# One root chain for two pieces of 256 tokens: 20 pairs of head norms in a hybrid decoder layer on one core

## The chip, the core and the metric

The kernel runs on one core of one Trainium2 chip. The metric is the device time of one execution in microseconds (us): the median of 3 runs is 1681.12 us (1680.39 to 1683.96).

## What is computed

One decoder layer over 2048 tokens of width 1024, in fp32. The normalised input is projected at once into the columns of five head groups (A: spatial gating, B: forgetting attention, C: mLSTM, D: RWKV-7, M: attention into 256 memory tokens), each group is mixed along the tokens, gated, and all are projected back. Four of the five use RMS norms over heads of 64 columns:

```python
def rms_norm(x, g):
    xf = x.astype(jnp.float32)
    y = xf * lax.rsqrt(jnp.mean(xf * xf, axis=-1, keepdims=True) + EPS)
    return (y * g.astype(jnp.float32)).astype(x.dtype)

q = rms_norm(to_heads(q), q_g)          # groups B and M; k likewise
v = rms_norm(to_heads(gelu(v)), norm_g) # group A
h = sigmoid(o_logit) * h                # group C, the mLSTM's output
return rms_norm(h, out_g).reshape(bsz, seq, GROUP_W)
```

With 4 heads of 64 in each group, a piece of 256 tokens (two blocks of 128 on the partitions, 256 columns each) needs 8 roots per partition: 2 blocks by 4 heads.

## The kernel before, in words

**Work.** The tokens go in four quarters q of 512 (Q). Weights come by DMA (tile wraw) and are split by ScalarE and VectorE into a high and a low fp32r half (wt); the input comes the same way (xr, then ht). A projection is 3 matmuls for each of 8 slices of 128 rows. `proj_tok` (line 647) makes one piece of 256 tokens in one PSUM bank (tag pj): 48 matmuls, shown as pj<-wt,ht 128x256. `proj_tok2` (634) makes both pieces side by side in two banks, 96 matmuls. `proj_T` (600) makes transposed tiles, shown as pj<-ht,wt 128x512, 24 matmuls per bank. There are 3 pj banks until about 942 us and 2 behind that.

**Order of the work.** The program is written by Python generators. A projection calls `tick()` after every few matmuls; a tick moves each generator in the crowd `evac` (class at line 86) by one step and each lane (RWKV front and back, mLSTM, gates, attention) by its rate, for the mLSTM 0.8 steps per tick. `evac.add(g, kind)` lets at most two generators of a kind live; for a third it ticks the crowd, without matmuls, until one has ended. Until about 942 us (L235 in the rows) the framework's scheduler then orders the instructions of each engine; behind that (L373) the kernel's own recorder does, by a list schedule (`flush`, 307). On every engine the instructions run in the order that results.

**The head norms.** `head_norm` (733) is one generator per piece: ScalarE squares the piece (tile sq), VectorE (DVE) sums each head's 64 squares (TENSOR_REDUCE rs<-sq), scales and adds eps (TENSOR_SCALAR rs<-rs), and `rsqrt` (487) takes the roots: a first guess by integer arithmetic (rq<-rs) and three Newton rounds of three instructions each on the tiles rq, the last one writing rs. These are 11 instructions on 8 columns, each waiting for the one before. After three more steps the caller multiplies the piece by the roots.

**Its four callers.** `qk_post` (748) for Bk, Bq and Mq: the piece is copied from its bank into a tile yn (2 buffers), normed, transposed by TensorE (wk<-ident,yn, 4 matmuls), copied back into yn with the gain, and stored (qk_Bk<-yn and so on). `mem_keys`, one piece, goes the same way. `gate_values` (1050) norms the two pieces of gv. `mlstm_block` (1964) norms its output H (tile to) after chunk 1 and after chunk 3, then transposes it (wk<-ident,to) and multiplies it into cgz. All in all 41 chains: 16 of Bk and Bq, 8 of Mq, 1 of the memory keys, 8 of gv, 8 of the mLSTM.

**Around the end of a quarter** `group_B` (983) runs Bz, Bv, Bk, Bq. During Bq the next quarter's input is reloaded and split (xr<-hbd, ht), and the next quarter begins with `proj_T` of Cqk0. Bq's copies into yn need the two buffers that Bk's pieces held until their stores.

Of the kernel before, what the change touches and what calls it, by code (L numbers as in the profile page):

```python
# [9 lines left out]
F32 = mybir.dt.float32  # L10
F32R = mybir.dt.float32r
I32 = mybir.dt.int32
AF = mybir.ActivationFunctionType
ALU = mybir.AluOpType
AX = mybir.AxisListType
# [3 lines left out]
P = 128  # L19
# [4 lines left out]
HD = 64  # L24
# [3 lines left out]
EPS = 1e-6  # L28
Q = 512
# [35 lines left out]
class Lane:  # L65


    def __init__(self, rate=1.0):
        self.q, self.rate, self.due = deque(), rate, 0.0
# [390 lines left out]
def body(ctx: ExitStack, tc, x, xT, mem, memT, wp, wkv, wout, pv, wa, sguT, sgub, out, dbg=None):  # L460
    nc = rec = Recorder(tc.nc, tc)
# [25 lines left out]
    def rsqrt(t):  # L487

        n, b = t.shape[0], t.base_partition() if callable(t.base_partition) else t.base_partition
        y, u = (cp.tile([P, 16], F32, tag=f"rq{i}", bufs=1, name="rq")[b:b + n, :t.free_size()] for i in range(2))  # L490
        V.tensor_scalar(y.bitcast(I32), t.bitcast(I32), -0.5, 1597463007.0, op0=ALU.mult, op1=ALU.add)
        for o in (y, y, t):
            V.tensor_tensor(u, y, y, op=ALU.mult)
            V.scalar_tensor_tensor(u, u, -0.5, t, op0=ALU.mult, op1=ALU.mult)
            V.scalar_tensor_tensor(o, u, 1.5, y, op0=ALU.add, op1=ALU.mult)
# [234 lines left out]
        yield free  # L730
        then()

    def head_norm(pt, n, eps, pool=None):

        sq = pool.tile([P, 3 + Q], F32, tag="cext", bufs=2, name="sq") if pool else xp.tile([P, 512], F32, tag="sq", bufs=2, name="sq")
        A.activation(sq[:, :n], pt, AF.Square)
        yield
        m = n // HD
        r = xp.tile([P, 8], F32, tag="rs", bufs=4, name="rs")
        V.tensor_reduce(r[:, :m], sq[:, :n].rearrange("q (u x) -> q u x", x=HD), axis=AX.X, op=ALU.add)  # L740
        V.tensor_scalar(r[:, :m], r[:, :m], 1.0 / HD, eps, op0=ALU.mult, op1=ALU.add)
        rsqrt(r[:, :m])
        yield
        yield
        yield
        return r[:, :m].rearrange("q (u o) -> q u o", o=1).to_broadcast([P, m, HD])

    def qk_post(y, scale, d):

        r = yield from head_norm(y, 512, EPS)  # L750
        y3 = y.rearrange("q (u x) -> q u x", x=HD)
        V.tensor_tensor(y3, y3, r, op=ALU.mult)
        yield
        pt = bank()
        for p in range(2):
            for ii in range(2):
                T.transpose(pt[:, (2 * p + ii) * P:(2 * p + ii + 1) * P], y[:, ii * 256 + p * P:ii * 256 + (p + 1) * P], ident)
        A.activation(y, pt, AF.Copy, scale=scale)
        yield
        SY.dma_start(d.rearrange("p q t -> q p t"), y.rearrange("q (p t) -> q p t", p=2))  # L760

    def qk_cols(wt, hts, scale, dst, pts=None):
        def post(pt, d):
            y = xp.tile([P, 512], F32, tag="yn", name="yn")
            A.copy(y, pt)
            yield FREE
            yield from qk_post(y, scale, d)

        for i in range(0, 4, 2):
            evac.add(post(pts[i // 2] if pts else proj_tok(wt, hts, i), dst(i)), "yn")  # L770

# [233 lines left out]
    for q in range(NQ):  # L1005
        tok = slice(q * Q, (q + 1) * Q)
        hts = got()


        lanes["mlstm"].drain()  # L1010
        qk, gz = [None] * 4, []
        va = sp.tile([P, 4, NH, HD + 1], F32, tag="va", bufs=1, name="va")
        G.memset(va[:, :, :, HD:HD + 1], 1.0)
        to = sp.tile([P, 4, 256], F32, tag="to", bufs=1, name="to")
        for nm in GC:
            wt = W(nm)
            for j in range(2):
                if nm == "Cv":
                    A.copy(va[:, 2 * j:2 * j + 2, :, 0:HD].rearrange("q i u x -> q (i u) x"), proj_tok(wt, hts, 2 * j).rearrange("q (u x) -> q u x", x=HD))
                    evac.held -= 1  # L1020
                elif nm == "Co":
                    A.activation(to[:, 2 * j:2 * j + 2].rearrange("q i x -> q (i x)"), proj_tok(wt, hts, 2 * j), AF.Tanh, scale=0.5)
                    evac.held -= 1
                elif nm == "Cz":
                    gz.append(sp.tile([P, Q], F32, tag=f"cgz{j}", bufs=1, name="cgz"))
                    evac.add(gate(proj_T(wt, j, hts), gz[j]))
                else:
                    m = 2 * (nm == "Cqk1") + j
                    qk[m] = sp.tile([P, Q], F32, tag=f"qk{m}", bufs=1, name="qk")
                    evac.add(conv(proj_T(wt, j, hts), m, qk[m]))  # L1030
        lanes["mlstm"].q.append(evac.then(mlstm_block(nc, q, sp, xp, bank, ident, qk, va, to, gz, mcol, cdb, nmd, wid, cst, hp2, mixd[2], head_norm)))
        group_B(q)


# [12 lines left out]
        V.scalar_tensor_tensor(o, t_, 1.0, pt, op0=ALU.add, op1=ALU.mult)  # L1047
        yield FREE

    def gate_values(pt, o):  # L1050
        yield from gelu2(pt, o)
        v3 = o.rearrange("q (u x) -> q u x", x=HD)
        r = yield from head_norm(o, 512, 4 * EPS)
        V.tensor_tensor(v3, v3, r, op=ALU.mult)

    def spatial(pt, u_, gv, p, d):
# [44 lines left out]
    for q in (NQ - 1, 0, 1, 2):  # L1101
        tok = slice(q * Q, (q + 1) * Q)
        if q < NQ - 1:
            hts = got()
            group_M(q)
        if q == NQ - 1:
            while ahead and next(ahead[-1][2], ahead) is not ahead:
                pass
            while evac.all or any(l.q for l in lanes.values()):
                evac.tick()  # L1110
                for l in lanes.values():
                    l.step()
            csp.close()
            rctx.close()
            psx.close()
            ps = psx.enter_context(tc.tile_pool(name="ps2", bufs=1, space=PSUM))
            nbank = {"pj": 2, "wk": 3, "p2": 2, "acc": 1}
            rec.start()
            ctx.enter_context(tc.manual_schedule())
            att.open()  # L1120

            fu = [Unit(att, True, h, g) for h in range(NH) for g in range(NQ)]
            mu = [Unit(att, False, h, g) for g in range(NQ) for h in range(NH)]
            lanes["fox"].q.append(att.run(fu[:-1] + mu[:NH] + fu[-1:] + mu[NH:]))
            sp = cw.enter_context(tc.tile_pool(name="sp2", bufs=1))
            stage.update(pool=sp, bufs=2, raw=4, lag=2)
            wop = cw.enter_context(tc.tile_pool(name="wop", bufs=1))

            sgw = mp.tile([P, NH, P], F32, name="sgw")
            SY.dma_start(sgw, sguT)  # L1130
            G.affine_select(sgw, sgw, pattern=[[0, NH], [1, P]], compare_op=ALU.is_ge, fill=0.0, base=0, channel_multiplier=-1)
            sgb = mp.tile([P, 2, 1, P], F32, name="sgb")
            for p in range(2):
                for h in range(2):
                    SY.dma_start(sgb[64 * h:64 * h + 64, p, 0, :], sgub[2 * p + h:2 * p + h + 1, :].to_broadcast([64, P]))
            V.tensor_scalar(sgb, sgb, 0.25, None, op0=ALU.mult)


        wt = W("Av")
        gv = sp.tile([P, 2, 512], F32, tag="gv", name="gv")  # L1140
        for i in range(2):
            evac.add(gate_values(proj_tok(wt, hts, 2 * i), gv[:, i]), "gl")
        wt = W("Au")
        gu = []
        for p in range(2):
            gu.append(sp.tile([P, 512], F32, tag=f"gu{p}", name="gu"))
            evac.add(gelu2(proj_T(wt, p, hts), gu[p]), "gl")
        wt = W("Az")
        if q == NQ - 1:
            evac.add(mem_rstd(), "gl")  # L1150
        pts = proj_T2(wt, hts, send(load_mem, "mem_g", NMEM) if q == NQ - 1 else reload(q + 1) if q != NQ - 2 else None)
        for p in range(2):
            evac.add(spatial(pts[p], gu[p], gv, p, mixd[0][p][:, tok]), "gl")
        if q == NQ - 1:
            hm = got()
            evac.add(mem_keys(proj_tok2(W(0), hm, None, 2)[0]), "yn")
            evac.add(mem_values(proj_tok2(W(1), hm, reload(0), 2)[0]), "gl")
# [803 lines left out]
    A.copy(mcol.rearrange("q k x -> q (k x)"), pt[:, 0:192])  # L1961


def mlstm_block(nc, q, sp, xp, bank, ident, qk, va, to, gz, mcol, cdb, nmd, wid, st, hp2, mixd, head_norm):

    V, A, G, T, SY = nc.vector, nc.scalar, nc.gpsimd, nc.tensor, nc.sync
    tokq = slice(q * Q, (q + 1) * Q)
# [19 lines left out]
    for c in range(4):  # L1987
# [48 lines left out]
            V.tensor_tensor(H4[:, h], num[:, h, :, 0:64], dn[:, h].to_broadcast([P, 2, HD]), op=ALU.mult)  # L2036
        V.scalar_tensor_tensor(H[:, c], to[:, c], 1.0, hr, op0=ALU.add, op1=ALU.mult)
        if c % 2:
            h2 = H[:, c - 1:c + 1].rearrange("q c x -> q (c x)")
            h3 = h2.rearrange("q (u x) -> q u x", x=HD)  # L2040
            r = yield from head_norm(h2, 512, 4 * EPS, sp)
            V.tensor_tensor(h3, h3, r, op=ALU.mult)
        yield
    yield
    for p in range(2):
        pt = bank()
# [67 lines left out]
```

## Time and profile before

| | |
|---|---|
| median of 3 runs | 1681.12 us |
| profiled execution, own time / span | 1675.38 us / 1673.7 us |
| TensorE matmul (PE) busy | 1607.7 us, 96% of the span |
| VectorE (DVE) busy | 1198.6 us, 72% |
| ScalarE (ACT) busy | 858.0 us, 51% |
| GpSimd (POOL) busy | 316.5 us, 19% |
| mean granted TensorE clock | 0.988 |
| chain that ended last, by engine | PE 71%, DVE 13%, DMA 8% |

Busy time says how full an engine is, not whether anyone waits for it. The views used further down are: busy time by stretch of the span (with the granted TensorE clock), the list of who waited for whom, the summary of one tile's instructions, and single instructions in order of time, where a bracket at the end gives the idle time of the engine before the instruction and what ended it. The tile names in the rows carry no buffer numbers.

### The profile page before, as it was taken

How to read it: one execution, taken by the hardware profiler on the slowest of the kernel's cores; microseconds unless marked ns; L12 is line 12 of the kernel's file. 1: busy time of each engine (PE TensorE's matmuls, PEld its weight loads, DVE VectorE, ACT ScalarE, POOL GpSimd, SP SyncE). 2: the span in 40 equal slices, each digit the busy share in tenths (PEclk: the TensorE clock that was granted, in tenths of full speed). 3: DMA queues.
4: the chain of work that ended last, by engine and by line, in shares of the span. 5: the costliest groups of instructions: out<-in, count | busy, mean ns of one | idle time of the engine just before them, and what ended most of it. 6: DMA issues, size and time to landing. Idle time of an engine off the chain costs nothing.

```text
span 1673.7 us, 31662 instructions
## 1 busy us (share of the span) xinstructions
PE 1607.7 (96%) x11306; PEld 1282.1 (77%) x11306; DVE 1198.6 (72%) x2990; ACT 858.0 (51%) x1838; POOL 316.5 (19%) x357
## 2 busy tenths in 40 slices
PE   7898999999999999998999999999999999999999
PEld 5676778787988887887898867777777775777887
DVE  7678686785886778579677688788878889753321
ACT  5576564654554455345545576556556657432110
POOL 5010001010000101001100034346354334010000
PEclk9998999999999999999999999999999999999999
DMA  6778654642453435335232646435333445744432
GB/s 200 242 243 256 186 169 146 159 140 73 138 171 101 129 102 166 101 99 161 80 111 83 182 134 184 104 83 146 100 107 108 140 107 149 217 124 127 134 122 76
DMA packets 200150, 234.35 MB, mean 140 GB/s; under 512 B 75016, under 2 KB 107336, under 8 KB 199992
## 3 DMA queue, kind: packets, MB, share of 16 engines
q1 hardware_dynamic: 185144, 218.69, 44.7%
q10 hardware_dynamic: 14848, 13.64, 2.7%
q8 instruction: 89, 1.46, 0.4%
q14 instruction: 69, 0.57, 0.1%
HBM read 180.44 MB, written 51.81 MB: 139 GB/s over the span
## 4 chain that ended last, share of the span: by engine, by line
PE 71%; DVE 13%; DMA 8%; issue 3%; ACT 3%; POOL 1%; SPq 0%; ACTq 0%; DVEq 0%; POOLq 0%
PE pj L235 26%; PE pj L373 23%; PE rw L235 6%; PE wk L235 5%; PE wk L373 4%; PE p L373 4%; PE acc L373 4%; DMA xr<-hbd 2%; DVE wt L235 1%; DVE rq L235 1%; DVE ht L373 1%; DVE ht L235 1%; DVE mx L373 1%; DMA wraw<-in_wp 1%; DVE wt L373 1%
## 5 line engine op out<-in xcount | busy, mean ns | idle before, releaser
L235 PE MATMUL pj<-ht,wt 128*128 128x512 f32 x1648 | 426.8, 407 | 21.6 <-ACT wt L235 14.8
L235 PEld LDWEIGHTS pj<-ht,wt 128*128 128x128 f32 x1648 | 305.7, 192 | 95.3 <-ACT wt L235 15.2
L235 PE MATMUL pj<-wt,ht 128*128 128x256 f32 x2016 | 271.8, 288 | 0.0
L235 PEld LDWEIGHTS pj<-wt,ht 128*128 128x128 f32 x2016 | 249.7, 191 | 6.9 <-ACT cext L235 0.4
L235 DVE TENSOR_TENSOR wt<-wraw,wt 128x512 fp32r<-128x512 f32 (+1 forms) x236 | 159.0, 676 | 45.4 <-ACT wt L235 43.8
L235 ACT CAST wt<-wraw 128x512 fp32r<-128x512 f32 (+1 forms) x236 | 139.2, 595 | 85.9 <-PE pj L235 52.0
L373 POOL TENSOR_TENSOR es<-es,pe 128x512 f32<-128x512 f32 (+3 forms) x128 | 161.5, 1262 | 111.1 <-ACT pe L373 105.4
L373 PE MATMUL pj<-ht,wt 128*128 128x512 f32 x528 | 141.0, 398 | 0.2 <-DVE gv L373 0.2
L373 DVE TENSOR_REDUCE mx<-wk 128x1 f32<-128x512 f32 (+3 forms) x192 | 113.4, 615 | 32.5 <-PE wk L373 31.3
L373 ACT ACTIVATE pe<-p 128x512 f32<-128x512 f32 x192 | 100.0, 542 | 54.0 <-PE p L373 45.1
L373 PEld LDWEIGHTS pj<-ht,wt 128*128 128x128 f32 x528 | 96.5, 189 | 23.3 <-issue 3.5
L373 PE MATMUL pj<-wt,ht 128*128 128x256 f32 x768 | 109.5, 288 | 3.8 <-DVE ht L373 2.2
L373 PEld LDWEIGHTS pj<-wt,ht 128*128 128x128 f32 x768 | 101.2, 192 | 13.7 <-issue 5.0
L373 PE MATMUL acc<-pe,v 128*64 128x512 f32 (+3 forms) x384 | 94.8, 562 | 2.5 <-DVE at L373 1.6
L373 DVE TENSOR_TENSOR xr<-pj,xr 128x512 f32<-128x512 f32 x32 | 22.1, 691 | 104.1 <-PE pj L373 103.9
L373 PE MATMUL pj<-ht,mt 128*128 128x512 f32 x384 | 94.9, 395 | 0.0
L373 POOL TENSOR_TENSOR es<-pe 128x512 f32<-128x512 f32 (+1 forms) x32 | 43.7, 1366 | 227.6 <-ACT pe L373 196.3
L373 PEld LDWEIGHTS pj<-ht,mt 128*128 128x128 f32 x384 | 71.5, 188 | 16.5 <-issue 0.6
L373 ACT CAST mt<-mr 128x256 fp32r<-128x256 f32 x80 | 31.6, 406 | 98.0 <-DVE xr L373 50.8
L373 PE MATMUL p<-qa,kb 128*128 128x512 f32 x192 | 74.9, 391 | 4.2 <-ACT pe L373 4.2
L373 DVE TENSOR_TENSOR wt<-wraw,wt 128x512 fp32r<-128x512 f32 x82 | 68.9, 851 | 12.2 <-ACT wt L373 12.0
L373 PE MATMUL p<-qb,ka 68*128 68x512 f32 x192 | 75.2, 393 | 0.0
(324 smaller groups left out, 2786.2 us busy)
## 6 DMA issues: line engine op xcount, KB each, us to landing
wraw<-in_wp SPq DMA_DIRECT2D x288, 256.0 KB
xr<-hbd SPq DMA_DIRECT2D x56, 256.0 KB
mr<-mix SPq DMA_DIRECT2D x80, 128.0 KB
xr<-in_x SPq DMA_DIRECT2D x32, 256.0 KB
out<-xr ACTq DMA_DIRECT2D x32, 256.0 KB
xt<-in_x SPq DMA_DIRECT2D x24, 256.0 KB
xr<-in_xT SPq DMA_DIRECT2D x24, 256.0 KB
hbd<-xr SPq DMA_DIRECT2D x24, 256.0 KB
```

What stands on the lines that cost most here:

```text
L235: getattr(getattr(self.nc, eng), fn)(*a, **k)
L373: getattr(getattr(self.nc, o.eng), o.fn)(*o.a, **o.k)
```

## The change

A class `Pair` holds one tile for two pieces, 16 columns. Each piece is squared and summed as before, into its own 8 columns. The second piece that is summed takes the roots of both at once, on 16 columns; the first waits, a step at a time, until that is done. The memory keys keep a chain of their own. The mLSTM sums after chunks 1 and 3, takes the roots behind chunk 3 and multiplies both halves there, so that its generator has three steps fewer (18 for 21).

```diff
-    def head_norm(pt, n, eps, pool=None):
-        sq = ...
-        A.activation(sq[:, :n], pt, AF.Square)
-        yield
-        m = n // HD
-        r = xp.tile([P, 8], F32, tag="rs", bufs=4, name="rs")
-        V.tensor_reduce(r[:, :m], sq[:, :n].rearrange("q (u x) -> q u x", x=HD), axis=AX.X, op=ALU.add)
-        V.tensor_scalar(r[:, :m], r[:, :m], 1.0 / HD, eps, op0=ALU.mult, op1=ALU.add)
-        rsqrt(r[:, :m])
-        yield
-        yield
-        yield
+    class Pair:
+        def __init__(self):
+            self.n, self.ready = 0, False
+            self.r = xp.tile([P, 2, 8], F32, tag="rs", bufs=3, name="rs")
+
+        def squares(self, pt, pool=None):
+            sq = ...
+            A.activation(sq[:, :512], pt, AF.Square)
+            self.n += 1
+            n = self.n
+            yield
+            V.tensor_reduce(self.r[:, n - 1], sq[:, :512].rearrange("q (u x) -> q u x", x=HD), axis=AX.X, op=ALU.add)
+
+        def roots(self, eps, n=2):
+            r = self.r[:, :n].rearrange("q i u -> q (i u)")
+            V.tensor_scalar(r, r, 1.0 / HD, eps, op0=ALU.mult, op1=ALU.add)
+            rsqrt(r)
+            self.ready = True
+
+    def head_norm(pt, eps, pair=None):
+        one = pair or Pair()
+        i = one.n
+        yield from one.squares(pt)
+        if not pair or i:
+            one.roots(eps, i + 1)
+        while not one.ready:
+            yield
+        yield
+        yield
+        yield
+        return one.of(i)
...
     def qk_cols(wt, hts, scale, dst, pts=None):
...
-            yield from qk_post(y, scale, d)
+            yield from qk_post(y, scale, d, pair)
+        pair = Pair()
         for i in range(0, 4, 2):
...
-            evac.add(gate_values(proj_tok(wt, hts, 2 * i), gv[:, i]), "gl")
+            evac.add(gate_values(proj_tok(wt, hts, 2 * i), gv[:, i], pair), "gl")
...
 def mlstm_block(...):
...
         if c % 2:
-            h2 = H[:, c - 1:c + 1].rearrange("q c x -> q (c x)")
-            h3 = h2.rearrange("q (u x) -> q u x", x=HD)
-            r = yield from head_norm(h2, 512, 4 * EPS, sp)
-            V.tensor_tensor(h3, h3, r, op=ALU.mult)
-        yield
+            if c == 1:
+                pair = Pair()
+            yield from pair.squares(H[:, c - 1:c + 1].rearrange("q c x -> q (c x)"), sp)
+        yield
+    pair.roots(4 * EPS)
+    yield
+    yield
+    yield
+    for i in range(2):
+        h3 = H[:, 2 * i:2 * i + 2].rearrange("q c (u x) -> q (c u) x", x=HD)
+        V.tensor_tensor(h3, h3, pair.of(i), op=ALU.mult)
     yield
```

The change also moves instructions on every engine from the first paired norm on. Two engines at the end of the first quarter show it. On TensorE, from the end of the RWKV helper (wk<-bones,ag) through the rest of Bk (24 of the pj<-wt,ht) and Bq (96 of them); - is the order before, + the order now:

```order
 L235 MATMUL wk<-bones,ag 128x2 x4
-L235 MATMUL pj<-wt,ht 128x256 x60
-L235 MATMUL wk<-ident,yn 128x128 x4
+L235 MATMUL pj<-wt,ht 128x256 x24
+L235 MATMUL wk<-ident,to 128x128 x4
+L235 MATMUL pj<-wt,ht 128x256 x2
+L235 MATMUL wk<-ident,to 128x128 x4
+L235 MATMUL pj<-wt,ht 128x256 x34
+L235 MATMUL wk<-ident,rn 64x128 x8
 L235 MATMUL pj<-wt,ht 128x256 x60
```

The transposes of the mLSTM's output (to) now stand at the start of Bq, those of the RWKV norms (rn) within it, and Bk's first piece (yn) is no longer transposed there. The order of TensorE goes on, behind Bq, with the next quarter's Cqk0 (pj<-ht,wt):

```order
 L235 MATMUL pj<-ht,wt 128x512 x11
-L235 MATMUL wk<-ident,rn 64x128 x8
-L235 MATMUL wk<-ident,to 128x128 x8
-L235 MATMUL pj<-ht,wt 128x512 x28
+L235 MATMUL wk<-ident,yn 128x128 x4
+L235 MATMUL pj<-ht,wt 128x512
 L235 MATMUL wk<-ident,yn 128x128 x4
 L235 MATMUL wk<-th,rkb 128x256 x2
```

Both pieces of Bk are now transposed 11 and 12 matmuls into Cqk0, where before the first was done in the middle of Bq and the second 39 matmuls into Cqk0. On ScalarE, at the same place, the rows now from the copy back of Bk's transposed pieces (yn<-wk) to the copies of Bq's pieces out of their banks (yn<-pj):

```order
L235 ACTIVATE yn<-wk,pvt 128x512
L235 ACTIVATE ht<-xr,pvt 128x512
L235 DMA xd<-xs 256x1x32 x4
L235 ACTIVATE yn<-wk,pvt 128x512
L235 ACTIVATE ht<-xr,pvt 128x512
L235 COPY yn<-pj 128x512
L235 ACTIVATE sq<-yn 128x512
L235 COPY cext<-pj 128x512
L235 ACTIVATE qk<-cext,pvt 128x512
L235 COPY yn<-pj 128x512
```

Before, Bq's first copy stood far ahead of the second yn<-wk, and its second copy seven rows behind it; now both copies follow both pieces of Bk closely.

## Rows read from the trace of the kernel before

**Rows 1.** The page, span and part 1: busy us, share of the span, instructions.
```profile
span 1673.7 us, 31662 instructions
PE 1607.7 (96%) x11306; PEld 1282.1 (77%) x11306; DVE 1198.6 (72%) x2990; ACT 858.0 (51%) x1838; POOL 316.5 (19%) x357
```

**Rows 2.** Windows: from:to length, PE, PEld, DVE, ACT, POOL busy (instructions), PE clock, DMA share, GB/s.
```profile
280.00:942.00 662.00, 642.71 (x5996) 548.16 (x5995) 487.70 (x1523) 337.99 (x755) 60.00 (x112) 1.00 0.43 123
942.00:1400.00 458.00, 444.84 (x2606) 330.97 (x2605) 386.11 (x728) 283.76 (x542) 199.01 (x160) 0.99 0.45 125
```

**Rows 3.** Who waited for whom, PE, 280 to 1400 us: total us, times, longest.
```profile
PE wk L235 <- DVE rn L235: 5.7, 3, 2.6
PE wk L235 <- DVE yn L235: 3.4, 4, 1.3
...
PE wk L373 <- DVE mx L373: 3.1, 3, 1.6
PE pj L235 <- ACT ht L235: 2.5, 2, 1.7
PE pj L373 <- DVE ht L373: 2.2, 3, 1.1
...
PE wk L373 <- DVE mm L373: 1.4, 1, 1.4
PE rw L235 <- DVE gt L235: 1.3, 2, 1.0
PE wk L235 <- DVE rq L235: 1.0, 1, 1.0
...
PE wk L235 <- DVE to L235: 0.7, 1, 0.7
```

**Rows 4.** Windows again: the ends of the first three quarters.
```profile
435.00:490.00 55.00, 51.48 (x463) 45.75 (x462) 51.95 (x184) 30.85 (x62) 6.16 (x12) 1.00 0.59 176
585.00:640.00 55.00, 52.34 (x505) 46.01 (x505) 36.83 (x110) 29.91 (x69) 2.70 (x8) 1.00 0.45 129
745.00:800.00 55.00, 50.69 (x487) 44.15 (x487) 51.30 (x187) 30.55 (x62) 6.78 (x11) 1.00 0.54 158
```

**Rows 5.** Tile rq: ns min/median/max of two forms, on 8 and on 16 columns.
```profile
L235 DVE SCALAR_TENSOR_TENSOR rq<-rq,rs x78: 143/163/174, 282.0 to 928.9; 128x8 f32<-128x8 f32 x78
...
L235 DVE SCALAR_TENSOR_TENSOR rq<-rq,sy x24: 168/173/176, 216.4 to 923.9; 64x16 f32<-64x16 f32 x24
```

**Rows 6.** Timeline of DVE: start us, us, instruction; a chain between other work.
```profile
452.29 0.16 DVE L235 SCALAR_TENSOR_TENSOR rq<-rq,rs 128x8 f32<-128x8 f32 x1
452.37 0.21 DVE L235 TENSOR_TENSOR xtmp<-xs,at 128x60 f32<-128x60 f32 x1
```

**Rows 7.** Timeline of DVE: a chain by itself.
```profile
321.77 0.17 DVE L235 SCALAR_TENSOR_TENSOR rq<-rq,rs 128x8 f32<-128x8 f32 x1
321.98 0.17 DVE L235 SCALAR_TENSOR_TENSOR rq<-rq 128x8 f32<-128x8 f32 x1
```

**Rows 8.** Timeline of DVE and PE: the end of gv's first chain, PE's wait for mm.
```profile
1370.34 0.17 DVE L373 SCALAR_TENSOR_TENSOR rs<-rq 128x8 f32<-128x8 f32 x1
...
1371.72 0.43 PE L373 MATMUL wk<-identr,mm 128*68 128x128 f32 x4 [1.37 <-DVE mm L373]
```

**Rows 9.** Timeline of PE and ACT: Bk's second piece handed over to Bq's second.
```profile
478.79 0.60 PE L235 MATMUL wk<-ident,yn 128*128 128x128 f32 x4
...
484.26 0.59 ACT L235 COPY yn<-pj 128x512 f32<-128x512 f32 x1 [0.77 <-DMA qk_Bk<-yn]
```

**Rows 10.** Timeline of PE, ACT: the pace of proj_T, and a wait of ACT for the reload.
```profile
315.36 7.76 PE L235 MATMUL pj<-ht,wt 128*128 128x512 f32 x33
...
475.73 0.72 ACT L235 ACTIVATE ht<-xr,pvt 128x512 fp32r<-128x512 f32 x1 [4.01 <-DMA xr<-hbd]
```

**Rows 11.** Windows: the three us behind PE's longest wait for rn.
```profile
355.00:358.00 3.00, 2.63 (x18) 2.20 (x19) 2.54 (x10) 0.63 (x1) 0.00 (x0) 0.52 0.28 87
```

More of the change, by code (lines that the diff above doesn't have):

```diff
@@ L731, in gate, with of @@
         then()
-    def head_norm(pt, n, eps, pool=None):
-        sq = pool.tile([P, 3 + Q], F32, tag="cext", bufs=2, name="sq") if pool else xp.tile([P, 512], F32, tag="sq", bufs=2, name="sq")
-        A.activation(sq[:, :n], pt, AF.Square)
-        yield
-        m = n // HD
-        r = xp.tile([P, 8], F32, tag="rs", bufs=4, name="rs")
-        V.tensor_reduce(r[:, :m], sq[:, :n].rearrange("q (u x) -> q u x", x=HD), axis=AX.X, op=ALU.add)
-        V.tensor_scalar(r[:, :m], r[:, :m], 1.0 / HD, eps, op0=ALU.mult, op1=ALU.add)
-        rsqrt(r[:, :m])
+    class Pair:
[3 more added lines that the diff above has]
+        def squares(self, pt, pool=None):
+            sq = pool.tile([P, 3 + Q], F32, tag="cext", bufs=2, name="sq") if pool else xp.tile([P, 512], F32, tag="sq", bufs=2, name="sq")
+            A.activation(sq[:, :512], pt, AF.Square)
[8 more added lines that the diff above has]
+            self.ready = True
+        def of(self, i):
+            return self.r[:, i].rearrange("q (u o) -> q u o", o=1).to_broadcast([P, 8, HD])
+    def head_norm(pt, eps, pair=None):
[6 more added lines that the diff above has]
+            yield
         yield
@@ L745, in head_norm, with qk_post @@
         yield
-        return r[:, :m].rearrange("q (u o) -> q u o", o=1).to_broadcast([P, m, HD])
-    def qk_post(y, scale, d):
-        r = yield from head_norm(y, 512, EPS)
+        return one.of(i)
+    def qk_post(y, scale, d, pair=None):
+        r = yield from head_norm(y, EPS, pair)
         y3 = y.rearrange("q (u x) -> q u x", x=HD)
@@ L1030, in body @@
                     evac.add(conv(proj_T(wt, j, hts), m, qk[m]))
-        lanes["mlstm"].q.append(evac.then(mlstm_block(nc, q, sp, xp, bank, ident, qk, va, to, gz, mcol, cdb, nmd, wid, cst, hp2, mixd[2], head_norm)))
+        lanes["mlstm"].q.append(evac.then(mlstm_block(nc, q, sp, xp, bank, ident, qk, va, to, gz, mcol, cdb, nmd, wid, cst, hp2, mixd[2], Pair)))
         group_B(q)
@@ L1048, in gelu2, with gate_values @@
         yield FREE
-    def gate_values(pt, o):
+    def gate_values(pt, o, pair):
         yield from gelu2(pt, o)
         v3 = o.rearrange("q (u x) -> q u x", x=HD)
-        r = yield from head_norm(o, 512, 4 * EPS)
+        r = yield from head_norm(o, 4 * EPS, pair)
         V.tensor_tensor(v3, v3, r, op=ALU.mult)
@@ L1961, in gate_prep, with mlstm_block @@
     A.copy(mcol.rearrange("q k x -> q (k x)"), pt[:, 0:192])
-def mlstm_block(nc, q, sp, xp, bank, ident, qk, va, to, gz, mcol, cdb, nmd, wid, st, hp2, mixd, head_norm):
+def mlstm_block(nc, q, sp, xp, bank, ident, qk, va, to, gz, mcol, cdb, nmd, wid, st, hp2, mixd, Pair):
     V, A, G, T, SY = nc.vector, nc.scalar, nc.gpsimd, nc.tensor, nc.sync
@@ L2038, in mlstm_block @@
         if c % 2:
-            h2 = H[:, c - 1:c + 1].rearrange("q c x -> q (c x)")
-            h3 = h2.rearrange("q (u x) -> q u x", x=HD)
-            r = yield from head_norm(h2, 512, 4 * EPS, sp)
-            V.tensor_tensor(h3, h3, r, op=ALU.mult)
+            if c == 1:
+                pair = Pair()
+            yield from pair.squares(H[:, c - 1:c + 1].rearrange("q c x -> q (c x)"), sp)
         yield
+    pair.roots(4 * EPS)
[5 more added lines that the diff above has]
+        V.tensor_tensor(h3, h3, pair.of(i), op=ALU.mult)
     yield
```

## The prediction, made before the changed kernel was run

> **What bounds the kernel now.** I read the page first. TensorE is busy for 1607.7 of 1673.7 us [rows 1], and the change gives it the same matmuls, so all that can be won on it is the 66.0 us in which it stands still, and slow clock behind such a stand. VectorE, whose work the change cuts, is 72% busy [rows 1], a mean over unlike stages, so I took the windows next. The norms' chains begin at 282.0 us [rows 5]. From 280 to 942 us, where the framework orders the work, TensorE idles for 19.3 us; from 942 to 1400, under the kernel's recorder, for 13.2 [rows 2]. The other 33.5 lie ahead of the first norm and in the output projection, where there are none. So 32.5 us of idle time are within reach.
>
> Third, who TensorE waited for from 280 to 1400 us. The rows that VectorE ended are rn 5.7, yn 3.4, mx 3.1, ht 2.2, mm 1.4, gt 1.3, rq 1.0 and to 0.7, 18.8 us together [rows 3]; smaller ones are left aside. The norms' own products (yn, rq, to) are 5.1 of this. The rest is other work that came late because VectorE runs its queue in order. Fourth, where: the ends of the first three quarters have VectorE at 94%, 67% and 93% and TensorE idle for 3.5, 2.7 and 4.3 us [rows 4]. Those 165 us hold 10.5 of the 19.3; elsewhere in that stretch TensorE is nearly full whatever VectorE does, and VectorE's time is worth nothing.
>
> **What the change removes and adds on VectorE.** 40 of the 41 chains become 20: 440 instructions on 8 columns go, 220 on 16 come (the order of the changed kernel has just these counts). The 41 sums and the 41 products stay. The wider ones cost a little more: 173 ns against 163 for the same operation on 16 and 8 columns [rows 5], 220 times 0.01, 2.2 us. What a removed one frees depends on its neighbours. Between other work the next instruction starts 0.08 us behind it [rows 6]; in a chain by itself, 0.21 us [rows 7]. So the 220 fewer are worth 17.6 to 46.2 us of VectorE, less 2.2. That is not the gain; the gain is what TensorE's waits lose by it.
>
> **The sum, on TensorE's path.**
> - Own products, 5.1 us: two pieces used to be waited for one by one, and now once together. I take half, -2.5. Bounds: -5.1, if all of it goes, and 0 or worse, if the pair comes late (the first rival).
> - Other late work at the three quarter ends: idle of 10.5 us [rows 4], less the own products (nearly all of the 5.1 lies there) and less the 2.5 in which TensorE waited for ScalarE's half of ht [rows 3]; 2.9 are left. At each end stand Bk's two chains, Bq's two and one of the mLSTM; of the five, two stay, and the mLSTM's pair moves ahead. That takes away two chains or more, 22 instructions of 0.08, 1.8 us in front of what is late, more than a third of 2.9 at each. I take all, -2.9; bounds 0 and -2.9.
> - The recorder's stretch: mx, ht and mm, 6.7 us [rows 3]. Only the wait for mm comes straight behind a chain, that of gv's first piece, which ended 1.4 us ahead of the late matmul [rows 8]. I take -1.4, and 0 for the others; bounds 0 and -6.7.
> - Norms of Mq, of the last quarter and of the other gv: their results are stored or used long after, and TensorE is full; 0. If that cover went, a piece late by a tick of proj_T (6 matmuls) would cost 1.4 us at 0.235 [rows 10], once.
> - mLSTM: three steps fewer at 0.8 steps per tick end it about four ticks earlier; its transposes leave the crowded start of the next quarter. The wait for to is in the first line, and no more is taken.
> - The wait that is added: Bk's first piece now leaves its yn buffer with the second. Behind it queue its transposes on TensorE, Bk's store on SP and, on ScalarE, Bq's copy out of its bank, with all that ScalarE has behind that (sq, cext, wt). From the transposes to that copy took 5.5 us (478.79 to 484.26), and it was the store that ended the wait [rows 9]. Meanwhile Bq holds two of three banks. The new order leaves 13 matmuls of Cqk0 before a further bank is needed, 3.1 us at 0.235 [rows 10]. So TensorE would stand for up to 2.4 us at each of three quarter ends. Against it: TensorE cannot go faster there than ht arrives, and ScalarE waited 4.0 us for the reload at that very place [rows 10]. Between 0 and 2.4 I take 1.0 each, nearer the free end because of that wait: +3.0; bounds 0 and +7.2.
>
> Together -2.5 - 2.9 - 1.4 + 3.0 = **-3.8 us**. The profiled execution took 1675.38 us, of which the span is 1673.7, so this one would take 1671.6; it was 5.7 us faster than the median of the three runs. Against that median the forecast is 1681.1 - 3.8 = **1677.3 us**. Its own range is -1 to -9, so 1672 to 1680. A difference under 0.2% (3.4 us) can hardly be told from none here; the forecast stands just beyond that line.
>
> **The rivals.** *Slower, by the handover.* At each of the three quarter ends Bq waits for buffers that Bk now releases together. Price: 2.4 us a time by the bound above, and slow clock behind it: in the 3 us after TensorE's longest wait for rn (2.6 us [rows 3]) the granted clock was 0.52 [rows 11], nearly all at 1.2 instead of 2.4 GHz, which lost 1.4 us. Three times 3.8 is 11.4; the gain on the own products is lost, and 4.3 of the others stay: +7.1, 1688 us. It decides if the pair of yn is transposed less than 5.5 us of matmuls ahead of the next bank, as the order has it, and ht is not later still. For it: the place stands in the order. Against: the wait for the reload [rows 10], and that VectorE has less in front of the pair. The Trainium skill (Perfetto Trace Analysis, section Optimizing Scalar/DVE Operations) says that where Scalar or Vector isn't saturated but causes bubbles on other engines, breaking up instructions may let work complete sooner; this change merges them, and by that rule it would come out as this rival, at 1688. The trace has the rule's premise over the span (72%), but not at two of the three quarter ends (94% and 93%).
>
> *No change.* VectorE's time is freed where TensorE is full, and waits of other kinds (the reload, ScalarE's ht) take the places of those that go: 1681 us. For it: TensorE's 96%.
>
> *A larger gain.* VectorE's queue at the quarter ends and in the recorder's stretch, where it is busy for 386 of 458 us [rows 2], was what made rn, mx and ht late too; then two thirds of the 18.8 us go, with one stretch of slow clock: 12.5 + 1.4, about -14, 1667 us. Against it: most of those waits stand far from a norm.
>
> That the change does not do what it says is excluded by the order: 20 chains on 16 columns, one on 8.
>
> **How the numbers follow.** Forecast 0.45, larger gain 0.17, no change 0.15, slower 0.23. The forecast's own range is cut by the line of 3.4 us: 0.31 beyond it, 0.14 within. So faster 0.48, same 0.29, slower 0.23. Since the order of all engines changes behind 280 us, a single wait like the longest for rn, with its slow clock (2.6 and 1.4 us), can come or go anywhere, 4 us either way. The range reaches from the larger gain with 3 us beyond it, 1664, to just past the slower rival, 1689.
>
> **What would show it.** Right, if VectorE's busy time falls by some 15 to 45 us; if TensorE's waits for yn, rq and to sum to less than 4; if its idle time at the three quarter ends falls below 8; and if ScalarE's copies yn<-pj wait for Bk's store by no more than 2 us each. Wrong, if TensorE waits at the start of Cqk0 for yn or for a bank, with slow clock behind it, or if the time from 942 to 1400 us changes by more than 3 us, for which the sum has almost nothing.

## The result, and the profile after

The changed kernel took 1700.77 us (median of 4 runs, 1697.39 to 1704.15), the kernel before, run beside it, 1681.84 (1680.39 to 1683.96): a ratio of 1.0103, 95% interval 1.0062 to 1.0145. It is 1% slower, and 12 us above the end of the predicted range. The profiled execution took 1704.15 us. Its page, where the spans and busy times stand, against [rows 1]:

```profile
span 1702.4 us, 31473 instructions
PE 1622.6 (95%) x11306; PEld 1289.6 (76%) x11306; DVE 1179.4 (69%) x2770; ACT 859.7 (50%) x1838; POOL 315.3 (19%) x357
```

VectorE has just the 220 instructions fewer that were forecast, and is busy for 19.2 us less. But TensorE, with the same 11306 matmuls, is busy for 14.9 us more and idle for 13.8 us more (79.8 for 66.0). More busy time for the same matmuls is slow clock: its mean fell from 0.988 to 0.978 (0.977 to 0.979 in all four executions). So half of the 28.7 us by which the two profiled spans differ is standing still and half is running at a lower clock. Of these 28.7 some 10 us are scatter of single executions: the medians differ by 18.9, the profiled execution of before (1675.38) lies below all of those above, and that of the change is the longest of its four. The list of who waited for whom shows which waits came. It is over the whole span here ([rows 3] is from 280 to 1400 us, with the same columns); of TensorE's rows those that speak to the prediction:

```profile
PE acc L373 <- DVE at L373: 6.9, 3, 4.6
...
PE rw L235 <- DVE gt L235: 4.6, 7, 2.0
PE pj L235 <- DVE wt L235: 4.5, 4, 2.7
...
PE pj L373 <- DVE gv L373: 2.7, 1, 2.7
PE pj L373 <- DVE wt L373: 2.6, 1, 2.6
...
PE rw L235 <- ACT qv L235: 2.2, 1, 2.2
...
PE rw L235 <- ACT xb L235: 2.0, 2, 1.3
PE wk L235 <- DVE yn L235: 1.9, 2, 1.5
PE wk L235 <- DVE xs L235: 1.8, 2, 1.4
...
PE wk L235 <- DVE to L235: 0.2, 1, 0.2
```

And of the same list of the kernel before, where xb and xs do not occur:

```profile
PE rw L235 <- DVE gt L235: 1.9, 4, 1.0
PE acc L373 <- DVE at L373: 1.6, 1, 1.6
PE pj L235 <- DVE wt L235: 1.5, 1, 1.5
PE rw L235 <- ACT qv L235: 0.9, 1, 0.9
PE pj L373 <- DVE gv L373: 0.2, 1, 0.2
```

The waits for the norms' own products fell as meant: yn and to together 2.1, and rq is gone, for 5.1 before. What grew most are waits for things that are no part of a norm (at, wt, gt, qv, xb, xs). Only gv, 2.7 us for 0.2, is multiplied by roots.

**One wait, followed to its cause.** The transposes of rn that began at 355.37 us (just ahead of the stretch in [rows 11]) now begin at 365.76. Of these 10.4 us 0.9 were lost up to 260 us and 1.8 to slow clock (0.91) from 260 to 280, all ahead of the first norm, so that is scatter:

```profile
260.00:280.00 20.00, 19.77 (x108) 16.91 (x109) 13.58 (x40) 7.01 (x15) 0.15 (x1) 0.91 0.40 111
```

The other 7.7 us are in the main one event. TensorE in order of time, where the bracket is the idle time before an instruction and what ended it:

```profile
306.23 0.73 PE L235 MATMUL pj<-ht,wt 128*128 128x512 f32 x2
309.13 1.21 PE L235 MATMUL rw<-qv,gt 128*64 128x64 f32 x16 [2.16 <-ACT qv L235]
310.26 0.47 PE L235 MATMUL rw<-sv,rk 64*64 64x64 f32 x2
```

And the granted clock (the third number from the end) in stretches of 4 us behind it:

```profile
304.00:308.00 4.00, 2.97 (x20) 1.65 (x15) 1.96 (x4) 0.96 (x3) 0.00 (x0) 1.00 1.10 89
308.00:312.00 4.00, 2.87 (x27) 2.54 (x28) 1.30 (x3) 1.85 (x5) 0.00 (x0) 0.67 0.67 161
312.00:316.00 4.00, 4.00 (x18) 3.12 (x19) 1.90 (x5) 2.99 (x5) 0.82 (x1) 0.50 0.47 161
316.00:320.00 4.00, 4.00 (x19) 3.12 (x17) 2.77 (x4) 0.62 (x1) 0.58 (x2) 0.50 0.30 66
320.00:324.00 4.00, 4.00 (x18) 3.21 (x17) 3.04 (x8) 0.60 (x2) 0.29 (x1) 0.62 0.22 36
324.00:328.00 4.00, 4.00 (x21) 3.13 (x20) 2.83 (x11) 3.96 (x6) 0.00 (x0) 1.00 0.49 126
```

TensorE stood for 2.16 us and then ran at the lower of its two levels, 1.2 GHz, for some 14 us: 4 x (0.33 + 0.50 + 0.50 + 0.38) = 6.8 us lost to the clock, three times the wait. What was ScalarE doing?

```profile
304.47 0.55 ACT L235 COPY xc<-rw 64x128 f32<-64x128 f32 x2
308.06 0.72 ACT L235 ACTIVATE ht<-xr,pvt 128x512 fp32r<-128x512 f32 x1 [3.04 <-DMA xr<-hbd]
308.80 0.57 ACT L235 ACTIVATE qv<-rw 64x128 f32<-64x128 f32 x2
```

The copy qv, which TensorE needed, stood in ScalarE's queue behind the next ht, and that one waited 3.04 us for its reload. In the kernel before the same two instructions stand the other way round:

```profile
301.96 0.55 ACT L235 COPY xc<-rw 64x128 f32<-64x128 f32 x2 [0.18 <-PE rw L235]
302.41 0.62 ACT L235 CAST wt<-wraw 128x512 fp32r<-128x512 f32 x1
303.05 0.57 ACT L235 ACTIVATE qv<-rw 64x128 f32<-64x128 f32 x2
303.92 0.72 ACT L235 ACTIVATE ht<-xr,pvt 128x512 fp32r<-128x512 f32 x1 [0.30 <-DMA xr<-hbd]
```

Neither qv nor ht has to do with a norm. Mq's norms are late in the new order: a copy of yn out of wk, which ScalarE had at 300.58 us, comes at 333.86. Other instructions moved up, the ht among them.

### The profile page after: what moved, and what is told of

Read it like the earlier page. It is cut to its first block, busy times and chain, and to the rows that moved or that the text cites. A ratio compares the mean times of both kernels' runs of the same rounds, so it can differ in the third digit from the quotient of the medians.

```text
span 1702.4 us, 31473 instructions
## 1 busy us (share of the span) xinstructions
PE 1622.6 (95%) x11306; PEld 1289.6 (76%) x11306; DVE 1179.4 (69%) x2770; ACT 859.7 (50%) x1838; POOL 315.3 (19%) x357
## 4 chain that ended last, share of the span: by engine, by line
PE 69%; DVE 15%; DMA 9%; issue 3%; ACT 3%; POOL 1%; SPq 0%; ACTq 0%; DVEq 0%; POOLq 0%
PE pj L373 24%; PE pj L235 22%; PE rw L235 6%; PE acc L373 4%; PE wk L373 4%; PE wk L235 4%; PE p L373 4%; DMA wraw<-in_wp 2%; DVE wt L235 2%; DMA xr<-hbd 2%; DVE rq L235 1%; DMA xr<-in_xT 1%; DVE ht L235 1%; DMA xt<-in_x 1%; DVE xtmp L235 1%
## 5 line engine op out<-in xcount | busy, mean ns | idle before, releaser
L235 PE MATMUL pj<-ht,wt 128*128 128x512 f32 x1648 | 435.9, 412 | 23.0 <-ACT wt L235 13.0
L235 PE MATMUL pj<-wt,ht 128*128 128x256 f32 x2016 | 275.4, 289 | 0.0
L373 PE MATMUL pj<-ht,wt 128*128 128x512 f32 x528 | 142.4, 401 | 2.7 <-DVE gv L373 2.7
L373 PE MATMUL pj<-wt,ht 128*128 128x256 f32 x768 | 110.6, 289 | 5.2 <-DVE wt L373 2.6
L373 PE MATMUL acc<-pe,v 128*64 128x512 f32 (+3 forms) x384 | 98.5, 574 | 9.3 <-DVE at L373 6.9
```

The source lines that it names most:

```text
L235: getattr(getattr(self.nc, eng), fn)(*a, **k)
L373: getattr(getattr(self.nc, o.eng), o.fn)(*o.a, **o.k)
```

## The experiments

Where the ratio of a run is given, it is to the kernel before on the same chip, with its 95% interval; 1% is 16.8 us. The theories: **A**, the wait that the change adds is what costs (in the expectations of the first four runs A is narrower, the handover of Bk's buffers to Bq); **B**, the event at 309 us; **C**, any change of the order costs; **D**, the place of the norms' results in the order; **E**, a step taken up at another place of the emission. Profiles of single executions scatter: the stretch up to the third transposes of rn, which lies ahead of all norms, ended between 256.8 and 264.9 us in the 18 kernels. Where the text says how many matmuls of an order were moved, it is the fewest that have to be moved to turn TensorE's order in one trace into that in the other (equal ones count as the same).

### One part of the change at a time

The parts that are left out keep one chain per piece; the number of tiles for the sums changes with it in most of these runs (four of 8 columns and one of 16, for three of 16). For instance:

```diff
-        pair = Pair()
+        pair = Pair() if two else None
         for i in range(0, 4, 2):
```

The mLSTM alone:

> Only the mLSTM's two pieces share their roots (and its three steps fewer); Mq, Bk, Bq and gv keep a chain of their own each. The sum of the prediction has 0 here, so 1681 us. Theory A, the handover of Bk's pair to Bq: 0, since Bk and Bq are as before. Theory B, slow clock behind a late qv at the Mq norms, from 309 us on: 0 up to 335 us, and nothing later. Theory C, that every change of the order of all engines moves small waits with slow clock behind them, whatever it is meant to do: any time within 10 us of 1681, and not the sum of what the profile shows of its own products.

Measured 1.0022 (0.9990 to 1.0054): no difference that can be told. Bk and Bq alone:

> Only Bk and Bq have pairs. The prediction's sum: -2.5 - 2 + 3, so 1679 to 1681 us. Theory A (handover): most of the 19 us of loss stands here, 1688 to 1700 us, with waits of TensorE for yn or for a bank at the three quarter ends and half clock behind. Theory B: 0, since Mq is as before. Theory C: any time within 10 us of 1681, with the waits at places that no yn is in.

Measured 1.0055 (1.0027 to 1.0082), 9 us slower, but not by the handover: by the list of waits TensorE never waited for yn, and for cext, which frees a bank, 0.7 us once; its waits for VectorE's rn, ht and gt were longer (9.9, 4.7 and 3.6 us over the span, for 8.0, 1.8 and 1.9 before). Mq alone:

> Only Mq's four pairs. The prediction's sum: 0, 1681 us. Theory A: 0. Theory B: the copy qv comes 2 us late at 309 us and TensorE runs at half clock for some 14 us behind it, so +7 to +10 us, 1688 to 1691, all of it before 335 us. Theory C: within 10 us of 1681, and the wait at 309 us need not come back.

Measured 1.0034 (1.0007 to 1.0062), 6 us, where theory B wants 7 to 10. The event at 309 us is there again, as B wants, and from the third to the fourth transposes of rn it took 103.7 us (96.1 before):

```profile
308.29 0.87 PE L235 MATMUL rw<-qv,gt 128*64 128x64 f32 x16 [2.07 <-ACT qv L235]
```

gv alone:

> Only gv's four pairs. The order up to 930 us is that of the kernel before. The prediction's sum: -1.4, 1680 us. Theory A and B: 0. If the loss of 7.8 us behind 940 us comes from gv, it stands here in full: 1689 us, with the waits for gv (2.7) and for a wt (2.6) that the changed kernel showed. Theory C: a loss or a gain of up to 5 us, with the waits at other places than in the changed kernel.

Measured 0.9972 (0.9943 to 1.0001), perhaps faster. The waits for at (4.6) and wt (2.6) of the changed kernel are here too, and yet from the recorder's first matmul to the end it took 736.2 us, as before (736.0), where the changed kernel took 743.8. But single profiles cannot carry those 7.8 us: five kernels whose order in this stretch is that of before (mLSTM, Bk with Bq, Bq, Bk, the mLSTM's end) took from 732.6 to 745.1 in it.

The four parts sum to +0.83%, near the whole change's 1.03, though by their intervals the sum could be half a percent more or less. It suggests that the loss has no one place; it does not say why.

### The wait without the saving, the saving without the wait

```diff
-            r = self.r[:, :n].rearrange("q i u -> q (i u)")
-            V.tensor_scalar(r, r, 1.0 / HD, eps, op0=ALU.mult, op1=ALU.add)
-            rsqrt(r)
+            for i in range(n):
+                r = self.r[:, i]
+                V.tensor_scalar(r, r, 1.0 / HD, eps, op0=ALU.mult, op1=ALU.add)
+                rsqrt(r)
```

> The first piece of each pair waits for the second as in the changed kernel, but the roots are then taken in two chains on 8 columns, so VectorE saves nothing. The prediction's sum without its gains: +3, 1684 us. Theory A (the added wait is what costs): as the changed kernel or a little above it, 1698 to 1706 us, with the wait for qv at 309 us and half clock behind it. Theory C (any change of the order costs, since places where a transfer is waited for fall ahead of what TensorE needs): above 1681 but anywhere up to 1700, with the waits at places of its own.

Measured 1.0116 (1.0078 to 1.0154), the same loss as the change, with the wait for qv (1.7 us) and slow clock behind it. The saved chains, then, are worth nothing that can be told in this order. Now the saving alone:

```diff
-        if not pair or i:
-            one.roots(eps, i + 1)
-        while not one.ready:
-            yield
+        if not i:
+            one.roots(eps, 1)
         yield
         yield
         yield
-        return one.of(i)
+        return one.of(0)
```

> VectorE is spared the same 20 chains, and nothing waits: the second piece of each pair takes the roots of the first, so its own roots are left out. The prediction's sum without its added wait: -6.8, 1674 us. Theory A: 1674 to 1681 us, since the wait is gone. Theory C: no gain from 20 chains fewer that can be told from the moves of the order; 1676 to 1695 us, with waits for other producers than yn.

Measured 0.9964 (0.9943 to 0.9986): 6.1 us faster (2.4 to 9.6). Its page: VectorE 26.7 us less, TensorE as before.

```profile
PE 1607.4 (96%) x11306; PEld 1280.7 (77%) x11306; DVE 1171.9 (70%) x2770; ACT 860.0 (51%) x1838; POOL 310.1 (19%) x357
```

So far theory A stands: the saving gains what was forecast, and waiting loses it three times over. But the profile does not show the gain where the forecast had it: its span is 1673.7, as in the profile before, and TensorE still waited 5.0 us for yn and rq and 1.4 for mm (5.1 with to, and 1.4, before). Nor is it the saving in an order that stays: no step of the program moved, but of the 7390 matmuls ahead of the recorder's part 648 were moved in TensorE's order (1179 in the changed kernel).

### Steps moved, with no pair at all

The kernel before, with one `yield` more, or one less, behind the roots of `head_norm` (the tiles for the sums are as before in all kernels of this section):

```diff
         rsqrt(r[:, :m])
         yield
         yield
         yield
+        yield
```

> The kernel before, with each head norm's product one step of its evacuation (about one tick of a projection) later: the same instructions, no pair. The prediction's sum: 0, 1681 us. Theory A: 1681 us within 3. Theory C: the order of all engines shifts as it does in the changed kernel, so 5 to 15 us above 1681, with waits of TensorE at places that are not the norms' own.

Measured 1.0078 (1.0050 to 1.0107).

> The kernel before, with each head norm's product one step earlier: the same instructions, no pair. The prediction's sum: 0, 1681 us. Theory A: 1681 us within 3. Theory C: 5 to 15 us above 1681 or, less likely, below it, again at places that are not the norms' own.

Measured 1.0098 (1.0060 to 1.0135). The second is the blow to theory A: results that come *sooner* lose as much as the change does. The same instructions, 13 and 16 us slower, at places of their own (in the first, 7.8 us of waits for mx in place of 3.1). With only the norms of Mq, Bk, Bq and the memory's keys a step later (`yield` behind `head_norm` in `qk_post`):

> The kernel before, with the products of the norms of Mq, Bk, Bq and the memory's keys one step later; those of gv and the mLSTM stay. Theory A: 1681 us within 3. Theory D: most of what all norms one step later cost (13 us), since the results that TensorE transposes and SP stores are these: 1690 to 1695 us. Theory C: 5 to 15 us above 1681.

Measured 1.0030 (1.0007 to 1.0053): 5 us, where D wants 9 to 14. And steps that have nothing to do with a norm, the output gates':

```diff
         A.activation(o, pt, AF.Tanh, scale=0.5)
         yield
+        yield
         V.scalar_tensor_tensor(o, o, 1.0, pt, op0=ALU.add, op1=ALU.mult)
```

> The kernel before, with one step more between the tanh and the product of every output gate (Bz, Mz, Cz, Az); the norms are not touched. Theory D (only the place of the norms' results is sensitive): 1681 us within 3. Theory C (the order before is a lucky one among its neighbours, and any shift loses it): 5 to 15 us above 1681, TensorE's busy time up by 3 to 20 us through slow clock.

Measured 1.0069 (1.0043 to 1.0094): D falls, C still holds. And the place at 309 us was hit again, on another copy (x) behind a waiting ht, by 3.68 us. TensorE and ScalarE there:

```profile
311.85 2.07 PE L235 MATMUL rw<-rk,bk 64*128 64x128 f32 x8 [3.68 <-ACT x L235]
```

```profile
308.28 0.72 ACT L235 ACTIVATE ht<-xr,pvt 128x512 fp32r<-128x512 f32 x1 [3.35 <-DMA xr<-hbd]
310.25 0.72 ACT L235 ACTIVATE ht<-xr,pvt 128x512 fp32r<-128x512 f32 x1 [1.25 <-DMA xr<-hbd]
...
311.43 0.37 ACT L235 COPY x<-rw 64x256 f32<-64x256 f32 x1
```

The mLSTM's last part three steps later (three `yield`s more ahead of its last loop):

> The kernel before, with the mLSTM's last part (its two transposed products and their stores) three steps later in each quarter; the norms are not touched. Theory E: steps move, so 3 to 15 us above the kernel before. If moved steps as such cost nothing: within 3 us of it.

Measured 1.0027 (1.0003 to 1.0051), a small loss.

### A pair with almost nothing to wait for

In Bq of the first three quarters both pieces leave their matmuls together; in Bk they come one after the other.

> Pairs only for Bq of the first three quarters, whose two pieces leave their matmuls together, so that the first has almost nothing to wait for. Theory A (the added wait costs): no loss, 1678 to 1682 us. Theory D (what costs is that the norms' results come at another place of the order, early or late): 1678 to 1682 us too, since they hardly move. Theory C (any change of the order costs): 5 to 15 us above 1681.

Measured 1.0070 (1.0038 to 1.0103).

> Pairs only for Bk of all four quarters, whose first piece is ready half a projection ahead of the second. Theory A: the whole loss of the run with Bk and Bq, 1686 to 1692 us. Theory D: the same, by the move of the first piece. Theory C: 5 to 15 us above 1681. Handover of the prediction: waits of TensorE for yn or for a bank at the quarter ends, up to 2.4 us each.

Measured 1.0063 (1.0040 to 1.0085). Theory A wanted no loss in the first and has lost here too; the second fits A, C and D alike. Where the first one's profile lost most, the wait was for xc of the RWKV part, 1.59 us at 501 us, and the clock behind it (columns as above):

```profile
500.00:510.00 10.00, 8.57 (x49) 6.53 (x50) 4.41 (x15) 3.34 (x9) 0.19 (x1) 0.68 0.04 15
510.00:520.00 10.00, 10.00 (x70) 8.74 (x71) 3.74 (x7) 3.32 (x9) 0.00 (x0) 0.50 0.35 106
520.00:530.00 10.00, 10.00 (x76) 6.49 (x75) 1.52 (x3) 3.54 (x10) 0.00 (x0) 0.79 0.13 38
```

10 x (0.32 + 0.50 + 0.21) = 10.3 us of clock behind 1.6 us of standing. This profile (span 1709.7) is that kernel's slowest execution, 17 us above its median, but shows what such a stretch can cost.

### Work that grows or shrinks in place

The head norms with two rounds of Newton's rule, and with four:

```diff
-        for o in (y, y, t):
+        for o in (y,) * (rounds - 1) + (t,):
```

> The kernel before, with two steps of Newton's rule for the head norms in place of three: 123 instructions on 8 columns fewer on VectorE, and nothing waits or moves by a step. This leaves out the last step of these roots. By the run that spared 20 whole chains (220 instructions, 6 us): -3.5 us, 1677 to 1678 us. Theory C: any time from 1676 to 1695 us.

Measured 0.9983 (0.9967 to 1.0000), 3 us.

> The kernel before, with four steps of Newton's rule for the head norms in place of three: 123 instructions on 8 columns more on VectorE, no step of the program moved against another. Theory C as it stood (any change of the order of the queues costs): 5 to 15 us above the kernel before. Theory E (what costs is that a step is taken up at another place of the sequence in which the steps are emitted; work that only grows or shrinks in place costs or gives its own few us): the opposite of the two-step run, +2 to +5 us.

Measured 1.0050 (1.0027 to 1.0072), 8.4 us for 123 instructions more, while 123 fewer gave 3. This lies in C's range and above E's, though the interval (4.5 to 12.1) still touches E's 2 to 5; between C and E the run does not decide by its time.

The traces say more. In the runs with two and with four rounds 561 and 476 of the 7390 matmuls were moved, with 648 where whole chains were spared: about as many as in the kernels with moved steps that lost (243 with Mq's, Bk's and Bq's norms later, 785 with all norms sooner). So C, as a rule that any change of the order costs, does not hold: two of these three came out faster or no slower, and so did the pairs of gv, which move 144 of the recorder's 3916. In the three the time goes with VectorE's work (220 and 123 instructions fewer, 6.1 and 3 us; 123 more, 8.4), and what the order has in it cannot be read off. What is left of E is that moved steps cost; four rounds cost too, without one.

### Mending the one place, and turning the knob

The changed kernel, with only Mq's first two pieces unpaired (`two=q < NQ - 1` in `group_M`):

> The changed kernel, but with Mq's first two pieces (the ones at 280 us) on a chain of their own each. Theory B (there ScalarE's next ht, which waits for its reload, comes ahead of the copy qv): no wait for qv at 309 us, the granted clock from 300 to 340 us is 1.00 again, and the transposes of rn start within 2 us of the kernel before, at 355 to 357 us in place of 365.8; the total is 1691 to 1694 us. Theory C: the stretch up to 355 us is mended as well, but what comes behind is a new order, so the total is anywhere from 1683 to 1705 us.

Measured 1.0072 (1.0047 to 1.0098). The place is mended: qv again stands ahead of the ht that waits, now for 1.83 us and with nobody behind it,

```profile
300.54 0.57 ACT L235 ACTIVATE qv<-rw 64x128 f32<-64x128 f32 x2
302.94 0.73 ACT L235 ACTIVATE ht<-xr,pvt 128x512 fp32r<-128x512 f32 x1 [1.83 <-DMA xr<-hbd]
```

the clock is 1.00 there,

```profile
300.00:320.00 20.00, 19.22 (x124) 14.99 (x124) 16.24 (x40) 12.21 (x21) 1.17 (x4) 1.00 0.67 146
320.00:340.00 20.00, 19.18 (x134) 16.75 (x132) 15.32 (x48) 13.46 (x31) 3.15 (x5) 1.00 0.65 166
```

and from the third to the fourth transposes of rn it took 97.2 us (354.01 - 256.81), as before the change (96.1) and not as after it (105.5). So B is the cause there. The total mended by less (1697.3 us, and its interval overlaps that of the whole change): from there to the recorder's first matmul it took 598.9 us in this profile, for 592.8 in the changed kernel and 582.3 before. What came behind lost more than it had.

> The changed kernel, with one step behind the roots of a pair in place of three (the mLSTM's keeps three), so that the first piece's product moves by less. Theory D: part of the loss comes back, 1688 to 1696 us. Theory C: no relation; 1680 to 1705 us.

Measured 1.0085 (1.0060 to 1.0110): moving the first piece's product back by two steps regains nothing that can be told.

> Pairs for gv alone, and two steps of Newton's rule for all head norms: the two edits that came out lowest, together. This leaves out the last step of these roots. If the gains are the edits' own and add up: 0.9972 times 0.9983, 0.9955, 1674 us. Theory C: the order is a new one again; 1675 to 1695 us.

Measured 0.9980 (0.9952 to 1.0008): the two gains do not add up, and no version here is below the kernel before beyond doubt, except the one whose second pieces take the roots of the first.

## Why the prediction was wrong

**What held.** The counts; VectorE's 15 to 45 us (19.2); the waits for yn, rq and to below 4 (2.1); and, by number, the gains: -6.8 us forecast for the saved work, 6.1 (2.4 to 9.6) measured where no step was moved. The number is luck in part: there the waits for yn, rq and mm, 3.9 of the 6.8, had not fallen. The handover was over-priced at +3.0: ScalarE's copies did wait for Bk's store, three times, 3.9 us in all and at most 1.70, which kept the 2 us asked for, and TensorE never stood for it. What it stood for at the start of Cqk0 was the late pair itself, once, with the clock at 1.00 behind it:

```profile
802.04 0.63 PE L235 MATMUL wk<-ident,yn 128*128 128x128 f32 x4 [1.47 <-DVE yn L235]
```

So the slower rival named the right side by a mechanism that hardly occurred, 1.5 us for the 11.4 of its price. The Trainium skill's rule on breaking up instructions (Perfetto Trace Analysis, section Optimizing Scalar/DVE Operations) also pointed to the right side; but merging the instructions is not what cost, since the pair taken in two chains lost as much as the merged one.

**The step that failed** is the last one: "Since the order of all engines changes behind 280 us, a single wait like the longest for rn, with its slow clock (2.6 and 1.4 us), can come or go anywhere, 4 us either way". It was taken as a scatter about zero, and of one event. It was a cost, and the largest term: against a saving of some 6 us the kernel lost 17 (1.0103 of 1681). Ten kernels moved steps ahead of 940 us without being the whole change: five with pairs for a part (mLSTM, Bk with Bq, Bk, Bq, Mq) and five with no pair at all (norms later, norms sooner, Mq's, Bk's and Bq's norms later, gates, the mLSTM's end). All ten came out slower, by 0.2 to 1.0%, nine of them with an interval above 1. That the order is another one is not enough for a loss, as the runs that only spare work show. The waits in the list differ from kernel to kernel, and no one resource stands out.

**The line on Mq** failed with it: "TensorE is full; 0", and 1.4 us once if the cover went. The place took some 7.7 us more, by an instruction that the line does not name. The working followed the norms' own results and asked who waits for those. It did not ask what the scheduler puts into the places that they leave, nor which instruction of the same queue waits for a transfer.

**A reading that was short.** The list of VectorE's waits called those that it left aside smaller; at, 1.6 us, and gz, 1.6, were larger than four that it took in. And at grew to 6.9.

**The price of slow clock** was too low: 1.4 us a wait, from the 3 us behind one wait [rows 11]. Behind qv it was 6.8. Between the two profiles TensorE's busy time grew by 14.9 us, more than its idle time.

**Two of the signs came out against the forecast.** TensorE's idle time at the three quarter ends was to fall below 8 us; in the stretches that answer to [rows 4] it is 12.3 (165 - 152.70, before 10.5):

```profile
445.00:500.00 55.00, 48.54 (x432) 42.70 (x430) 47.55 (x147) 29.66 (x59) 5.73 (x11) 0.97 0.59 170
598.00:653.00 55.00, 52.03 (x505) 46.61 (x504) 37.16 (x95) 27.46 (x60) 2.23 (x8) 0.97 0.45 121
761.00:816.00 55.00, 52.12 (x512) 45.86 (x509) 46.25 (x146) 27.44 (x57) 6.20 (x9) 1.00 0.55 158
sum 165.00, PE 152.70 PEld 135.17 DVE 130.96 ACT 84.56 POOL 14.16; mean PE 50.90 PEld 45.06 DVE 43.65 ACT 28.19 POOL 4.72
```

And the time from 942 to 1400 us was not to change by more than 3 us; the part from the recorder's first matmul to the end grew from 736.0 to 743.8, which lies within what equal orders scatter there.

**What stays open.** That steps moved ahead of 942 us cost here is shown; why all ten cost and none gains is not. One reading is that the order before has fewer bad places than its neighbours. For the place at 309 us that is seen: ht with its wait stands behind qv before and when only chains were spared, and it stands ahead of qv, or a second ht ahead of x, with half clock behind, in five kernels that moved steps (change, Mq, waiting pairs, pairs two steps sooner, gates). In most of the others that moved steps the clock there was 1.00, and they lost elsewhere. Nor is it safe in the order before: in the Bk and Bq run, where ScalarE's order there is still that of before, ht waited 1.95 us (0.30 before), x came 0.9 us late behind it, and the clock from 300 to 320 us was 0.79; with four rounds it was 2.82, 1.7 and 0.78. When the transfer lands varies from execution to execution; the order decides what hangs on it. The 7.8 us behind 958 us cannot be told from scatter.

## What to carry to other kernels

Where a scheduler orders in-order queues, price an edit in two terms: what it saves, and what its moved steps do to the order. Here the first, with the order as it then came out, was -6 us; moved steps alone cost from 5 to 16 us, and the pairs' waiting without the saving 20. Measure the second by itself, with a `yield` more or fewer that changes no work, before a result of 1% is put down to the edit. And look in each queue that TensorE depends on for an instruction that waits for a transfer: whatever the order puts behind it inherits the wait, so it belongs behind the small copies of a dependent chain, not ahead of them. At the one place where this was mended it gave back some 6 us there, but not in the total.

## What the hardware showed that was not expected

What a stand of TensorE costs goes by more than its length. Behind 2.16 us at 309 us the clock stayed low for some 14 us, behind 1.59 us at 501 us (the Bq run) for some 20; both times the RWKV chain's small matmuls (rw, 64x64 among them) were among what followed. Behind the 1.86 us for rn at 365.76 us, where none of them follows, the clock was 1.00 throughout:

```profile
360.00:380.00 20.00, 18.14 (x137) 16.66 (x136) 19.94 (x57) 9.52 (x17) 3.67 (x4) 1.00 0.39 122
```

And behind the longest one of the kernel before, 2.55 us for rn at 355.37, it was 0.52 for 3 us [rows 11] and 0.91 in the next three. What makes the difference was not tried.
